# The mixer's last product as two sets of seven block products in place of eight column tiles

## The chip, the cores and the metric

The kernel runs on one core of a Trainium2 chip. The metric is device time in microseconds (us). Of the kernel before, three runs are shown, with a median of 1166.98 us (1166.12 to 1167.22). One further execution, taken with the profiler, lasted 1166.18 us, of which the profile covers a span of 1164.1 us. All places below are in microseconds from the start of that span.

Five engines work side by side, each in the order of its own queue: TensorE (PE, with its weight loads as PEld), VectorE (DVE), ScalarE (ACT), GpSimd (POOL, which here mostly issues adding transfers) and SyncE (SP, which issues most loads). They wait for each other by semaphores.

## The reference

One transformer block over 512 tokens with 1024 features, all in float32: half a SwiGLU feed-forward step, a mixer, another half step, a norm. The mixer is where the change lies:

```python
merged = sigmoid(ga) * y_conv + sigmoid(gb) * y_gla   # y_gla = (...) @ w_out_gla
return merged @ w_o                                   # 512 x 1024 by 1024 x 1024
...
x = x + hybrid_mixer(rmsnorm(x, norm_mix_g), w_in, conv_w, ..., w_o)
x = x + 0.5 * swiglu(rmsnorm(x, norm_ffn2_g), ffn2_w_gu, ffn2_w_down)
```

So the product with w_o is followed at once by the residual sum into x, and by the norm that opens the second feed-forward step (FFN2), whose first product needs that norm's inputs.

## The kernel before, in words

Activations lie transposed: 128 features on the partitions, 512 tokens along the row, so x and the merged tensor are eight tiles of 128x512. To keep float32 accuracy, every operand is split in two float32r parts, high and low, and each product is made of three: high by high, high by low, low by high.

**Weights** come in units of at most 128x1024 through one stream (class `Weights`). `PLAN` lists the units, `STEPS` the order in which the products take them. SP loads a unit from HBM into one of ten slots `f0` to `f9` (`dma`, line 334). Some steps before its use, ACT writes its high part (`wh`, line 374) and DVE its low part (`wl`, line 375); there are three buffers of each. A unit has served when both are written, and its slot can be loaded again. A slot is chosen by the step up to which the slots are needed (`until`).

**Plain tiles.** `mm_group` (line 423) makes four tiles of 128 output features at once, `mm_single` (line 409) one; either way a tile of 128x512 takes 8 blocks of 128 inputs by 3 parts, 24 matmuls with 512 columns. Before the change, the w_o product is one group and then four single tiles, 8 tiles in all. Its operands `m_h`, `m_l` are written by `split_pair` (lines 1560 and 1561) as soon as the merged tensor is ready, its results go through `evac` (line 1662): x = result + the old x, which had been loaded into eight tiles `x_old` during the product with w_out_conv. After each tile `nxt.add` feeds FFN2's norm: ACT writes x times gain as high part (line 459) and the square (465, 468), DVE the low part (460) and the running sum of squares (469).

**Sets.** Most other products are made of sets of seven block products after Strassen and Winograd: the weights of 1024 inputs by 512 outputs are four blocks a11, a12, a21, a22, the operand is four blocks of 4 feature tiles by 256 tokens, and seven products of blocks (named m1, p2, q6, p5, q7, p4, p3) take the place of eight. A narrow product (`Product.narrow`, line 533) is 24 matmuls with 256 columns and takes one unit of weights. The sums of weight blocks are made in place: POOL's adding transfers do a21 += a22 first, a11 += a21 once the weights of m1 have been split, and a12 += a11 once those of p2 have been split; DVE makes s3 = a11 + a21 (line 361). The sums of operand blocks are made by DVE in place (lines 749 to 756), and each is split by `Both` (ACT line 623, DVE line 624, in two halves). The products pile up in three PSUM banks a, b, c per set; where a bank holds a finished quarter of the output, `done` takes it out, and the bank's next product has to wait for that. The product with w_out_gla is of this kind (two sets; the results are taken out by lines 609, 612, 1641 and 1645), and so are FFN2's.

**What sets the order.** The program is written product by product, with the weights of the next two or three steps being split ahead (`Weights(2)`), and with operands made two steps ahead in `run_sets`. A scheduler of the framework then orders each engine's queue; on the chip each engine follows its own.

Of the kernel before, what the change touches and what calls it, by code (L numbers as in the profile page):

```python
# [62 lines left out]
def unit_cols(u):  # L63
    return u[2] * len(u[3]) * u[4]
# [7 lines left out]

HW = 256


# [32 lines left out]

def sets(mat, pairs):
# [41 lines left out]
def mixer_plan():  # L151
# [28 lines left out]
def block_kernel(ctx: ExitStack, tc: tile.TileContext, xT, vecs, gf, gup, wgl, wts, out):  # L180
# [101 lines left out]
    class Weights:  # L282
# [3 lines left out]
        def __init__(self, ahead):  # L286
            self.ahead = ahead
            self.issued = 0
            self.taken = 0
            self.end = 0  # L290
            self.ready = []
            self.raw = {}
            self.loads = {}
            self.sums = {}
            self.first = {}

        def phase(self, early, first=6):


            self.early = early  # L300
            self.until = [-1] * SLOTS
            lo, self.end = self.end, [e for e in ENDS if e > self.end][0]
# [26 lines left out]
        def dma(self, n, until):  # L329
            u = PLAN[n]  # L330
            w = unit_cols(u)
            o = offset(n)
            t = self.slot(until)
            nc.sync.dma_start(t[:, :w], wts[o : o + P * w].rearrange("(p n) -> p n", p=P))
            return t

        def load_set(self, n):
# [16 lines left out]
        def issue(self):  # L354
# [192 lines left out]
    class Set:  # L547
# [52 lines left out]
        def quarter(self, p):  # L600
# [12 lines left out]
            return t  # L613

    class Both:

# [113 lines left out]
    class Operands:  # L730
# [4 lines left out]

        def __init__(self, b):
            self.b = b
            self.parts = {}
            self.sums = set()
# [20 lines left out]
        def make(self, p):  # L760
            if p in self.parts:
                return
            i = self.ORDER.index(p)
            if i > 0:
                self.make(self.ORDER[i - 1])
            v = self.sum(p)
# [377 lines left out]
    def mixer(norm, nxt):  # L1144
# [8 lines left out]

        Y = [tile_of("y", [P, 2, S + 2]) for _ in range(4)]

# [422 lines left out]
        def sigmoid(t):  # L1578
# [3 lines left out]

        c_h, c_l = parts([Y[i][:, :, 2:] for i in range(4)])
        m = [two(d // 2)[:, d % 2] for d in range(KD)]

# [9 lines left out]
        ga = [gate("ga", d) for d in range(2)]  # L1595
        x_old = [QK[2 + i][:, j] for i in range(2) for j in range(2)] + [
            pools["g"].tile([P, S], F32, tag=t, name=f"{t}_x") for t in ("sc", "reset", "gup_w", "glr")]
        gb_new = []
# [5 lines left out]
        for d in range(KD):  # L1604
# [24 lines left out]
        sigmoid(gb_new.pop())  # L1629
        m_h, m_l = [None] * KD, [None] * KD  # L1630

        def gla_done(i):
            def done(s, p):
                if not (i == 1 and p in ("q6", "p5", "q7")):
                    finish_late()
                if p not in QUARTERS:
# [6 lines left out]
                    op0=ALU.mult, op1=ALU.mult)  # L1643
                y = two(d // 2)
                nc.vector.tensor_tensor(out=y[:, :, half(l)], in0=y[:, :, half(l)], in1=pair(g),
                                        op=ALU.add)
# [11 lines left out]
        run_sets(lambda i: Set(oo, gla_done(i)), hooks={(0, "p3"): [reload]})  # L1658
        finish_late()

        def evac(d, o):
            nc.vector.tensor_tensor(out=x[d], in0=o, in1=x_old[d], op=ALU.add)
            nxt.add(d)

        for d, o in enumerate(mm_group("w_o", KD, (0, P, 2 * P, 3 * P), m_h, m_l)):
            evac(d, o)
        for d in range(4, KD - 2):
            evac(d, mm_single("w_o", KD, d * P, m_h, m_l))
        for d, o in [(d, mm_single("w_o", KD, d * P, m_h, m_l)) for d in range(KD - 2, KD)]:
            evac(d, o)  # L1670

    FFN = dict(f=1, hidw=2, hid=3, tp=9)
    with phase("small1", **FFN):
# [10 lines left out]
        ffn("ffn1_w_gu", "ffn1_w_down", n1, nm, PLAIN1, 5)  # L1684
    with phase("small2", f=1, v=4, qk=2, g=1, y=4, small=1):
        W.phase(4, 5)
# [49 lines left out]
```

## Time and profile before

| | |
|---|---|
| time of three runs, median | 1166.98 us |
| profiled execution: time, span | 1166.18 us, 1164.1 us |
| PE busy | 1155.0 us, 99% of the span |
| DVE, ACT, POOL busy | 956.7, 684.6, 117.7 us |
| granted clock of TensorE | 0.999 of full speed |
| w_out_conv (single tiles) | up to 739.14 |
| w_out_gla (14 narrow products) | 739.14 to 779.67 |
| w_o (8 tiles) | 779.67 to 823.21 |
| FFN2 begins | 823.21 |

How to read it: PE is the busy engine, and its rows follow each other nearly without a gap, so a stage lasts as long as its matmuls, plus what PE waits. A matmul's own duration is longer than the step from one to the next, since they are pipelined; steps, not durations, add up. The same holds on DVE and ACT, where an instruction starts a little before the one ahead has ended.

### The profile page before, as it was taken

The numbers are of one execution on the slowest core, as the hardware profiler recorded it, in microseconds if no ns is written. First come the engines' busy times: TensorE is split into PE (matmuls) and PEld (weight loads), VectorE is DVE, ScalarE is ACT, GpSimd is POOL, SyncE is SP. The second block draws the span as 40 slices with busy tenths as digits, with TensorE's granted clock in tenths as the row PEclk, the third lists the DMA queues.
The fourth block names the chain that finished last, engine by engine and source line by source line (L and its number), as shares of the span: only waits on it lengthen the run. The fifth ranks groups of instructions, "written<-read, shape, count | busy, mean of one in ns | idle before, by whom it ended". The sixth has DMA issues, their size and how long they took to land.

```text
span 1164.1 us, 17143 instructions
## 1 busy us (share of the span) xinstructions
PE 1155.0 (99%) x6626; PEld 1016.1 (87%) x6626; DVE 956.7 (82%) x1198; ACT 684.6 (59%) x904; POOL 117.7 (10%) x153
## 2 busy tenths in 40 slices
PE   9999999999999999999999999999999999999997
PEld 7898888988888889999989998998889888898886
DVE  7997888997568977979799998686599788889955
ACT  6466666675335656666666586544356666666443
POOL 0010111101020111100101100000001111111100
PEclk9999999999999999999999999999999999999999
DMA  9388787678524488876868767531738777757721
GB/s 350 79 212 195 178 201 180 163 193 204 207 80 122 106 200 230 197 188 171 224 169 207 211 171 221 134 107 52 227 74 209 182 187 177 196 145 183 184 86 73
DMA packets 62593, 200.11 MB, mean 172 GB/s; under 512 B 6864, under 2 KB 13136, under 8 KB 62512
## 3 DMA queue, kind: packets, MB, share of 16 engines
q1 hardware_dynamic: 39088, 126.37, 32.3%
q0 software_dynamic: 18784, 68.17, 31.8%
q10 hardware_dynamic: 4640, 4.49, 1.1%
q8 instruction: 52, 0.85, 0.3%
q14 instruction: 29, 0.24, 0.1%
HBM read 124.55 MB, written 8.39 MB: 114 GB/s over the span
## 4 chain that ended last, share of the span: by engine, by line
PE 96%; DVE 2%; ACT 1%; DMA 1%; issue 1%; ACTq 0%
PE mm L824 13%; PE mm L409 11%; PE mm L533 11%; PE bb L542 10%; PE z L542 8%; PE mm L423 8%; PE w L542 7%; PE y L542 6%; PE mm L1041 4%; PE aux L824 4%; PE x L542 3%; PE y L533 3%; PE w L533 2%; PE aux L1041 1%; PE z L533 1%; PE x L533 1%
## 5 line engine op out<-in xcount | busy, mean ns | idle before, releaser
L374 ACT CAST wh<-f 128x1024 fp32r<-128x1024 f32 (+1 forms) x341 | 356.0, 1047 | 339.6 <-PE mm L533 37.8
L375 DVE TENSOR_TENSOR wl<-f,wh 128x1024 fp32r<-128x1024 f32 (+1 forms) x341 | 413.6, 1217 | 98.4 <-ACT wh L374 89.3
L352 POOL DMA_DIRECT2D f<-f x126 | 109.0, 865 | 905.8 <-DVE wl L375 512.0
L824 PE MATMUL mm<-wh,op 128*128 128x512 f32 x432 | 106.9, 389 | 0.0
L533 PE MATMUL mm<-op,wh 128*128 128x256 f32 x800 | 105.6, 284 | 0.0
L533 PEld LDWEIGHTS mm<-op,wh 128*128 128x128 f32 x800 | 100.1, 192 | 0.5 <-ACT tp L583 0.2
L542 PE MATMUL bb<-op,wh 128*128 128x512 f32 x384 | 97.9, 395 | 0.0
L824 PEld LDWEIGHTS mm<-wh,op 128*128 128x128 f32 x432 | 80.9, 188 | 16.7
L409 PE MATMUL mm<-op,wh 128*128 128x512 f32 x384 | 91.0, 389 | 0.0
L409 PEld LDWEIGHTS mm<-op,wh 128*128 128x128 f32 x384 | 72.0, 188 | 15.0
L542 PEld LDWEIGHTS bb<-op,wh 128*128 128x128 f32 x384 | 69.4, 189 | 12.7
L542 PE MATMUL z<-op,wh 128*128 128x512 f32 x256 | 64.4, 393 | 0.0
L423 PE MATMUL mm<-op,wh 128*128 128x512 f32 x256 | 64.1, 392 | 0.2 <-DVE op L456 0.2
L824 PE MATMUL mm<-wl,op 128*128 128x512 f32 x216 | 57.7, 389 | 0.0
L423 PEld LDWEIGHTS mm<-op,wh 128*128 128x128 f32 x256 | 47.5, 188 | 10.9 <-ACT wh L374 0.5
L542 PEld LDWEIGHTS bb<-op,wl 128*128 128x128 f32 x384 | 52.3, 190 | 5.0 <-DVE wl L375 1.3
L533 PE MATMUL mm<-op,wl 128*128 128x256 f32 x400 | 56.5, 283 | 0.0
L542 PE MATMUL w<-op,wh 128*128 128x512 f32 x224 | 56.3, 393 | 0.0
L542 PE MATMUL bb<-op,wl 128*128 128x256 f32 x384 | 53.6, 282 | 0.9 <-DVE wl L375 0.9
L542 PEld LDWEIGHTS z<-op,wh 128*128 128x128 f32 x256 | 46.0, 189 | 8.2
L361 DVE TENSOR_TENSOR f<-f,f 128x1024 f32<-128x1024 f32 x42 | 51.3, 1222 | 1.6 <-DMA f<-wts 0.9
L533 PEld LDWEIGHTS mm<-op,wl 128*128 128x128 f32 x400 | 51.8, 192 | 0.3
(334 smaller groups left out, 2003.7 us busy)
## 6 DMA issues: line engine op xcount, KB each, us to landing
f<-wts SPq DMA_DIRECT2D x219, 512.0 KB, 4.5
f<-f POOLq DMA_DIRECT2D x126, 512.0 KB, 5.2
X<-xT SPq DMA_DIRECT2D x8, 256.0 KB, 5.4
xs<-X POOLq DMA_DIRECT2D x8, 256.0 KB, 2.4
tp<-ga SPq DMA_DIRECT2D x8, 256.0 KB, 5.6
y<-tp SPq DMA_DIRECT2D x7, 256.0 KB, 2.0
ga<-tp ACTq DMA_DIRECT2D x6, 256.0 KB, 3.9
gb<-tp ACTq DMA_DIRECT2D x6, 256.0 KB, 3.9
```

Of the source, the lines that this page charges most:

```text
L352: return nc.gpsimd.dma_start(out_, a, accum_op=ALU.add).ins
L361: nc.vector.tensor_tensor(out=s3, in0=a11, in1=a21, op=ALU.add)
L374: self.cast = nc.scalar.copy(h[:, :w], raw[:, :w]).ins
L375: nc.vector.tensor_tensor(out=l[:, :w], in0=raw[:, :w], in1=h[:, :w].bitcast(F32), op=ALU.subtract)
L409: nc.tensor.matmul(o, w[:, i * P : (i + 1) * P], a[k], start=j == k == 0, stop=j == 2 and k == kt - 1)
L423: nc.tensor.matmul(o[c], w[:, s : s + P], a[k], start=k == 0 and j == 0, stop=k == kt - 1 and j == 2)
L533: nc.tensor.matmul(o[:, e * HW : (e + 1) * HW], w[:, k * HW + e * P : k * HW + (e + 1) * P], a(k), start=self.fresh and j == k == e == 0, ...
L542: nc.tensor.matmul(o[:, e, :n], w[:, k * HW + e * P : k * HW + (e + 1) * P], a(k), start=self.fresh and k == 0 and w is self.h, stop=k == ...
L824: nc.tensor.matmul(o[t], a(k)[:, t * P : (t + 1) * P], ww[:, i * 512 : (i + 1) * 512], start=fresh and j == k == 0, stop=j == 2 and k == 3 ...
L1041: nc.tensor.matmul(o[t][e], b if j == 1 else a, wl if j == 2 else wh, start=k == K0 and e == 1 and j == 0, stop=k == KF - 1 and j == 2, sk ...
```

## The change

The w_o product becomes two sets of seven narrow products, of four output feature tiles (512 features) each, run in the same call of `run_sets` as the two sets of w_out_gla. `OUT_SEQ` writes out their order: (0, "m1") is the first product of the set for outputs 0 to 511, (1, "m1") that of the set for 512 to 1023. Both sets share their split operands `mo`, made from the merged tensor `MY`. `Straight` runs a product into its bank, copies b into a new bank a after m1, and hands every product's bank to `out_done`, which adds or subtracts it directly into a quarter of x (`X2`), which has been loaded there from `xs` (`reload`, now 8 loads during w_out_gla). After p3 a set's feature tiles 0 and 1 are complete, after p4 tiles 2 and 3, and `nxt.add` runs for two at a time. s3 is not summed by DVE: SP loads a11 a second time into s3's slot, and POOL adds a21 from HBM to it. Slots' `until` is kept between phases. Y's four tiles become one.

```diff
+BY_DMA = ("w_o",)
...
+OUT_SEQ = ((0, "m1"), (0, "p5"), (1, "m1"), (0, "p2"), (0, "q6"), (1, "p5"), (0, "q7"),
+           (0, "p3"), (0, "p4"), (1, "q6"), (1, "p2"), (1, "q7"), (1, "p3"), (1, "p4"))
...
-    STEPS.extend(order(firsts))
+    STEPS.extend([(firsts[i], p) for i, p in seq] if seq else order(firsts))
...
-    units(group("w_o", KD, (0, P, 2 * P, 3 * P)))
-    for d in range(4, KD):
-        units(single("w_o", KD, d * P))
+    sets("w_o", [(4 * i * P, (4 * i + 2) * P) for i in range(2)], OUT_SEQ)
...
-            s3 = self.slot(a["q7"])
+            s3 = self.dma(n, a["q7"]) if PLAN[n][0] in BY_DMA else self.slot(a["q7"])
...
-                nc.vector.tensor_tensor(out=s3, in0=a11, in1=a21, op=ALU.add)
+                if PLAN[n][0] not in BY_DMA:
+                    nc.vector.tensor_tensor(out=s3, in0=a11, in1=a21, op=ALU.add)
                 self.first[n] = self.add(a21, a22)
+                if PLAN[n][0] in BY_DMA:
+                    self.add(s3, self.block(n + 2))
...
+    class Straight:
+        BANK = {"m1": "b", "p2": "a", "q6": "b", "p5": "c", "q7": "b", "p4": "b", "p3": "c"}
...
+        def run(self, p):
+            n = self.BANK[p]
+            fresh = n not in self.bank
+            if fresh:
+                self.bank[n] = self.new(n)
+            Product(*W.take(), self.group.get(p), fresh).narrow(self.bank[n])
+            if p == "m1":
+                self.bank["a"] = self.new("a")
+                nc.scalar.copy(self.bank["a"], self.bank["b"])
+            self.done(p, self.bank[n])
...
-            nc.sync.dma_start(x_old[d], xs[d])
...
-                if p in ("p4", "p3"):
-                    def f():
-                        for j, (b, c) in enumerate(split_pair(y)):
-                            m_h[d + j], m_l[d + j] = b, c
-                    late.append(f)
...
+            for d in range(KD):
+                nc.sync.dma_start(x[d], xs[d])
+        mo = Operands(
+            lambda j, l: MY[:, 4 * j : 4 * j + 4, half(l)],
+            ("m1", "p5", "p2", "q6", "q7", "p3", "p4"))
+        def out_done(i):
+            def done(p, o):
+                if p == "m1":
+                    return
+                a = int(p in ("p5", "q7", "p4"))
+                l = int(p not in ("p2", "p4"))
+                d = 4 * i + 2 * a
+                v = XS[-1][:, d : d + 2, half(l)]
+                if a:
+                    nc.vector.scalar_tensor_tensor(out=v, in0=pair(o), scalar=-1.0, in1=v,
+                                                   op0=ALU.mult, op1=ALU.add)
+                else:
+                    nc.vector.tensor_tensor(out=v, in0=pair(o), in1=v, op=ALU.add)
+                if p in ("p3", "p4"):
+                    for e in range(2):
+                        nxt.add(d + e)
+            return done
+        def out_bank(i):
+            return lambda n: AUX() if (i, n) == (1, "b") else MM()
...
-        for d, o in enumerate(mm_group("w_o", KD, (0, P, 2 * P, 3 * P), m_h, m_l)):
-            evac(d, o)
-        for d in range(4, KD - 2):
-            evac(d, mm_single("w_o", KD, d * P, m_h, m_l))
-        for d, o in [(d, mm_single("w_o", KD, d * P, m_h, m_l)) for d in range(KD - 2, KD)]:
-            evac(d, o)
+        run_sets(out_set, hooks={(0, "p3"): [reload]})
```

The queues at three places. Line numbers are those of the kernel each row is from: 374, 375 of the kernel before are 384, 385 in the changed one, 459, 460, 468, 469 are 469, 470, 478, 479, and 623, 624 are 655, 656.

**PE at the end of w_o.** Before, the last tile's matmuls end and FFN2's group begins:

```order
L409 MATMUL mm1186_7830<-op1140_7503,wl1183_7772 128x512 x2
L409 MATMUL mm1186_7830<-op1125_7370,wl1183_7772 128x512 x2
L409 MATMUL mm1186_7830<-op1151_7580,wl1183_7772 128x512 x2
L409 MATMUL mm1186_7830<-op1149_7573,wl1183_7772 128x512 x2
L423 MATMUL mm1196_7898<-op1168_7708,wh1200_7902 128x512
```

Now, from the end of the eleventh product (1, p2), whose weights are wh1186 and wl1187 (aux1162 is bank b of the second set, mm1174 its bank c):

```order
L543 MATMUL mm1165_7694<-op1156_7624,wl1187_7874 128x256 x4
L543 MATMUL mm1174_7767<-op1172_7761,wh1194_7944 128x256 x4
L543 MATMUL mm1174_7767<-op1173_7764,wh1194_7944 128x256 x4
L543 MATMUL aux1162_7665<-op1168_7726,wh1192_7915 128x256 x4
L543 MATMUL aux1162_7665<-op1169_7729,wh1192_7915 128x256 x4
```

The first eight matmuls of the thirteenth product (1, p3) stand ahead of the twelfth, (1, q7). They need wh1194, the high part of a12 + a11 of the second set. That sum is the last adding transfer of w_o on POOL, and it can only be issued once wl1187 has been written from the same slot, f1131.

**DVE in the second half of w_o.** Before, at the sixth tile:

```order
L1662 TENSOR_TENSOR X2_7377<-mm1175_7733,sc_x_6749 128x512
L375 TENSOR_TENSOR wl1183_7772<-f1163_7648,wh1182_7771 128x1024
L460 SCALAR_TENSOR_TENSOR op1179_7764<-X2_7377,vec_84,op1178_7763 128x512
L469 TENSOR_TENSOR acc16_7707<-acc16_7707,tp1180_7767 128x512
L1662 TENSOR_TENSOR X2_7377<-mm1181_7770,reset_x_6750 128x512
```

Now, from (0, p3)'s result to (1, q6)'s:

```order
L1699 TENSOR_TENSOR X2_7368<-mm1157_7627,X2_7368 128x2x256
L385 TENSOR_TENSOR wl1187_7874<-f1131_7385,wh1186_7873 128x1024
L470 SCALAR_TENSOR_TENSOR op1184_7864<-X2_7368,vec_84,op1183_7863 128x512
L1696 SCALAR_TENSOR_TENSOR X2_7368<-mm1151_7589,X2_7368 128x2x256
L470 SCALAR_TENSOR_TENSOR op1184_7864<-X2_7368,vec_84,op1183_7863 128x512
L479 TENSOR_TENSOR acc16_7862<-acc16_7862,tp1185_7870 128x512
L385 TENSOR_TENSOR wl1193_7916<-f1130_7383,wh1192_7915 128x1024
L470 SCALAR_TENSOR_TENSOR op1189_7904<-X2_7368,vec_84,op1188_7903 128x512
L479 TENSOR_TENSOR acc16_7862<-acc16_7862,tp1190_7907 128x512
L470 SCALAR_TENSOR_TENSOR op1189_7904<-X2_7368,vec_84,op1188_7903 128x512
L479 TENSOR_TENSOR acc16_7862<-acc16_7862,tp1191_7912 128x512
L1699 TENSOR_TENSOR X2_7368<-aux1162_7665,X2_7368 128x2x256
```

The norm work of feature tiles 0 to 3 now stands in one block between two evacuations of banks.

**ACT from w_o into FFN2.** Before, FFN2's first two weight units (wh1200, wh1203) are cast ahead of the last two tiles' norm work:

```order
L459 ACTIVATE op1178_7763<-X2_7377,vec_84 128x512
L468 ACTIVATE tp1184_7802<-X2_7377 128x512
L374 CAST wh1200_7902<-f1191_7888 128x1024
L374 CAST wh1203_7908<-f1192_7890 128x1024
L468 ACTIVATE tp1189_7860<-X2_7377 128x512
```

Now they (wh1215, wh1218) stand behind the norm work of tiles 4 and 5, which needs the result of the thirteenth product:

```order
L384 CAST wh1194_7944<-f1131_7385 128x1024
L384 CAST wh1196_7973<-f1129_7381 128x1024
L469 ACTIVATE op1198_8027<-X2_7368,vec_84 128x512
L478 ACTIVATE tp1200_8031<-X2_7368 128x512
L469 ACTIVATE op1198_8027<-X2_7368,vec_84 128x512
L478 ACTIVATE tp1201_8036<-X2_7368 128x512
L384 CAST wh1215_8109<-f1206_8095 128x1024
L384 CAST wh1218_8115<-f1207_8097 128x1024
```

The cast of FFN2's first weights has moved from ahead of the last results to behind those of the thirteenth product.

More of the change, by code (lines that the diff above doesn't have):

```diff
@@ L613, in quarter, with __init__ @@
             return t
+    class Straight:
+        BANK = {"m1": "b", "p2": "a", "q6": "b", "p5": "c", "q7": "b", "p4": "b", "p3": "c"}
+        def __init__(self, group_, done, new):
+            self.group = group_
+            self.done = done
+            self.new = new
+            self.bank = {}
+        def run(self, p):
[8 more added lines that the diff above has]
+            self.done(p, self.bank[n])
     class Both:
@@ L1151, in mixer @@
             nc.gpsimd.dma_start(xs[k], x[k])
-        Y = [tile_of("y", [P, 2, S + 2]) for _ in range(4)]
+        YS = tile_of("y", [P, 4, 2, S + 2])
+        Y = [YS[:, i] for i in range(4)]
         def flat(i):
@@ L1583, in mixer @@
         c_h, c_l = parts([Y[i][:, :, 2:] for i in range(4)])
-        m = [two(d // 2)[:, d % 2] for d in range(KD)]
+        MY = YS.rearrange("p i e t -> p (i e t)")[:, : KD * S].rearrange("p (d t) -> p d t", t=S)
+        m = [MY[:, d] for d in range(KD)]
         n64 = [front.tile([P, HEADS * 16], F32, tag=t, name=f"{t}o") for t in
@@ L1595, in mixer @@
         ga = [gate("ga", d) for d in range(2)]
-        x_old = [QK[2 + i][:, j] for i in range(2) for j in range(2)] + [
-            pools["g"].tile([P, S], F32, tag=t, name=f"{t}_x") for t in ("sc", "reset", "gup_w", "glr")]
         gb_new = []
@@ L1656, in reload, with out_set @@
             x[:] = [XS[-1][:, k] for k in range(KD)]
[L1658 to L1663, printed above, removed]
-        for d, o in enumerate(mm_group("w_o", KD, (0, P, 2 * P, 3 * P), m_h, m_l)):
-            evac(d, o)
-        for d in range(4, KD - 2):
-            evac(d, mm_single("w_o", KD, d * P, m_h, m_l))
-        for d, o in [(d, mm_single("w_o", KD, d * P, m_h, m_l)) for d in range(KD - 2, KD)]:
-            evac(d, o)
+            for d in range(KD):
[22 more added lines that the diff above has]
+            return lambda n: AUX() if (i, n) == (1, "b") else MM()
+        def out_set(i):
+            if i < 2:
+                return Set(oo, gla_done(i))
+            return Straight(mo, out_done(i - 2), out_bank(i - 2))
+        run_sets(out_set, hooks={(0, "p3"): [reload]})
     FFN = dict(f=1, hidw=2, hid=3, tp=9)
@@ L1684, in block_kernel @@
         ffn("ffn1_w_gu", "ffn1_w_down", n1, nm, PLAIN1, 5)
-    with phase("small2", f=1, v=4, qk=2, g=1, y=4, small=1):
+    with phase("small2", f=1, v=4, qk=2, g=1, y=1, small=1):
         W.phase(4, 5)
```

28 lines of the change are left out of this document (14 added, 14 removed).

## The prediction

> **What bounds the kernel now.** I read the page's busy times first, then its chain that ended last.
>
> ```profile
> PE 1155.0 (99%) x6626; PEld 1016.1 (87%) x6626; DVE 956.7 (82%) x1198; ACT 684.6 (59%) x904; POOL 117.7 (10%) x153
> ...
> PE 96%; DVE 2%; ACT 1%; DMA 1%; issue 1%; ACTq 0%
> ```
>
> PE works for 99% of the span and makes 96% of the chain, so a change pays by what it takes from PE, less the waits that PE gets for it. Next, stretches of the program: engines' busy time, granted clock, DMA share and GB/s, for w_out_gla, for w_o, and for the mixer's earlier sets.
>
> ```profile
> core 0: us, PE busy (x) PEld busy (x) DVE busy (x) ACT busy (x) POOL busy (x), PEclk, DMA share, GB/s
> 739.10:779.70 40.60, 40.60 (x338) 40.39 (x338) 32.14 (x39) 21.33 (x27) 1.72 (x2) 1.00 0.54 148
> 779.70:823.20 43.50, 43.50 (x194) 36.02 (x193) 28.02 (x35) 19.08 (x25) 0.00 (x0) 1.00 0.30 109
> 640.00:699.00 59.00, 59.00 (x400) 54.73 (x399) 55.73 (x72) 41.46 (x53) 4.31 (x5) 1.00 0.70 189
> ```
>
> The clock is full in all three. In w_o DVE is idle for 15.5 of 43.5 us, POOL does nothing, and DMA is busy for 0.30. The last row matters too: sets kept DVE busy for 55.73 of 59 us there, and PE never stopped.
>
> **What the change takes from PE.** Rows of PE (start, duration) at both borders of w_o:
>
> ```profile
> 776.79 2.08 PE L533 MATMUL mm<-op,wh 128*128 128x256 f32 x16
> 778.71 1.12 PE L533 MATMUL mm<-op,wl 128*128 128x256 f32 x8
> 779.67 2.00 PE L423 MATMUL mm<-op,wh 128*128 128x512 f32 x8
> ...
> 801.45 3.79 PE L409 MATMUL mm<-op,wh 128*128 128x512 f32 x16
> 805.08 1.98 PE L409 MATMUL mm<-op,wl 128*128 128x512 f32 x8
> 806.89 3.79 PE L409 MATMUL mm<-op,wh 128*128 128x512 f32 x16
> 810.52 1.98 PE L409 MATMUL mm<-op,wl 128*128 128x512 f32 x8
> ...
> 823.21 1.98 PE L423 MATMUL mm<-op,wh 128*128 128x512 f32 x8
> ```
>
> A narrow product takes 779.67 − 776.79 = 2.88 us (24 matmuls, 120.0 ns apart), a plain tile 806.89 − 801.45 = 5.44 (226.7 ns apart). w_o goes from 823.21 − 779.67 = 43.54 = 8 × 5.44 to 14 × 2.88 = 40.32: **−3.22 us** if PE never waits. Not −5.44, as seven for eight would give: half the columns take more than half the time.
>
> The Trainium skill (TensorE: Matmul & The Clock Gate, section "Wait — 56ns, not 53.3ns?") gives a warm start-to-start of N ÷ 2.4 GHz plus about 2.5 ns: 109.2 and 215.8 ns here, so 336 × 109.2 = 36.7 against 192 × 215.8 = 41.4, and −4.7 us. The trace has 120.0 and 226.7, so the sum goes by the rows.
>
> **What it adds elsewhere.** Each unit of w_o's weights that is multiplied is split: 8 before, 14 now, so 6 more casts on ACT and 6 more low parts on DVE. The operands (8 splits of one tile before) are sums and `Both` splits now, and 12 results go into x where 8 did. All this lies beside PE's 40 us except where PE catches up with it. I looked for these places along the queues, from what is done at the border.
>
> **Stall 1, ahead of the thirteenth product (1, p3).** Its first eight matmuls stand ahead of the twelfth, and need the cast of a12 + a11. That sum is issued after wl1187 on DVE. DVE's steps, and the chain from an adding transfer to its cast, by the trace of before:
>
> ```profile
> 774.46 0.68 DVE L609 SCALAR_TENSOR_TENSOR tp<-mm,tp 128x512 f32<-128x512 f32 x1
> 775.18 0.69 DVE L1641 SCALAR_TENSOR_TENSOR g<-tp,g 128x512 f32<-128x512 f32 x1
> ...
> 779.33 1.21 DVE L375 TENSOR_TENSOR wl<-f,wh 128x1024 fp32r<-128x1024 f32 x1
> 780.46 0.68 DVE L1645 TENSOR_TENSOR y<-y,g 128x512 f32<-128x512 f32 x1
> 781.06 0.68 DVE L612 TENSOR_TENSOR tp<-mm,tp 128x512 f32<-128x512 f32 x1
> ...
> 804.87 0.75 DVE L460 SCALAR_TENSOR_TENSOR op<-X,vec,op 128x512 fp32r<-128x512 f32 x1
> 805.53 0.69 DVE L469 TENSOR_TENSOR acc<-acc,tp 128x512 f32<-128x512 f32 x1
> ```
>
> ```profile
> 767.37 0.86 POOL L352 DMA_DIRECT2D f<-f  x1 [16.71 <-DVE wl L375]
> 772.24 1.05 ACT L374 CAST wh<-f 128x1024 fp32r<-128x1024 f32 x1 [3.02 <-DMA f<-f]
> ```
>
> A step of 1024 columns is 780.46 − 779.33 = 1.13 us, one of 512 is 781.06 − 780.46 = 0.60 (0.72 where it reads what the one ahead wrote: 775.18 − 774.46), a norm low part 805.53 − 804.87 = 0.66. The instruction at 774.46 (the result of q7 of w_out_gla's second set) is the same in both kernels. From it up to and with wl1187, DVE's changed queue has 40 instructions: 14 of 1024 (11 low parts of weights, 3 operand sums) and 26 of 512 (10 that finish the GLA quarters, 10 low halves of operands, 6 evacuations). 14 × 1.13 + 26 × 0.60 = 31.42, plus 0.12 for the one dependent pair and 0.09 since the last counts with its whole 1.22: 774.46 + 31.63 = 806.09 if DVE never waits. PE has then 5.26 us left: eleven products end at 779.67 + 11 × 2.88 = 811.35.
>
> How long the add takes is the open price. Issue to landing in the trace (the last number; first the page's medians, with the loads of x beside them, then two single adds):
>
> ```profile
> f<-f POOLq DMA_DIRECT2D x126, 512.0 KB, 5.2
> X<-xT SPq DMA_DIRECT2D x8, 256.0 KB, 5.4
> ...
> f<-f POOLq DMA_DIRECT2D x1, 512.0 KB, 4.5
> ...
> f<-f POOLq DMA_DIRECT2D x1, 512.0 KB, 8.7
> ```
>
> The adds' median is 5.2; 4.5 is one at 861.6, in FFN2, and 8.7 one at 702.8, among the mixer's sets. The pair of rows above gives 772.24 − 767.37 = 4.87. I take the median: 806.09 + 5.2 + 1.05 (cast) + 0.04 = 812.38, a stall of **1.03 us**. Lower bound: with 4.5 the cast is ready at 811.68, but behind these eight matmuls (0.96) the twelfth product waits for its bank, which DVE frees behind wl1187, four norm low parts, one more weight part and four steps of 512: 806.00 + 4 × 0.66 + 1.13 + 4 × 0.60 + 0.69 = 812.86, against 811.35 + 0.96 = 812.31. So at least 0.55 even with a quick add. Upper bounds: with 8.7, 815.88 and 4.5 us; or, if every DVE instruction took its duration (1.22, 0.68) and not its step, 14 × 0.09 + 26 × 0.08 = 3.3 more, 4.4 us. The nearest row for the steps is the window 640 to 699, where DVE ran dense without a stall of PE; so the steps hold.
>
> **Stall 2, at FFN2's first matmul.** It waits for the cast wh1215, now behind the norm work of tiles 4 and 5, which need the thirteenth product's result. That chain, in rows of before (DVE, then ACT):
>
> ```profile
> 812.53 0.69 DVE L1662 TENSOR_TENSOR X<-mm,reset_x 128x512 f32<-128x512 f32 x1 [0.33 <-PE mm L409]
> ```
>
> ```profile
> 801.71 0.72 ACT L459 ACTIVATE op<-X,vec 128x512 fp32r<-128x512 f32 x1
> 802.33 0.62 ACT L465 ACTIVATE acc<-X 128x512 f32<-128x512 f32 x1
> 802.85 0.71 ACT L459 ACTIVATE op<-X,vec 128x512 fp32r<-128x512 f32 x1
> 803.46 0.62 ACT L468 ACTIVATE tp<-X 128x512 f32<-128x512 f32 x1
> 803.98 0.71 ACT L459 ACTIVATE op<-X,vec 128x512 fp32r<-128x512 f32 x1
> ...
> 813.26 0.72 ACT L459 ACTIVATE op<-X,vec 128x512 fp32r<-128x512 f32 x1 [2.17 <-DVE X L1662]
> ```
>
> A product's last matmul ends 778.71 + 1.12 − 779.67 = 0.16 after the next could start; its result reaches DVE 0.03 later (812.53 against 810.52 + 1.98); evacuation 0.69; 0.04 to ACT (813.26 against 812.53 + 0.69); four activations 803.98 − 801.71 = 2.27 (0.03 more for the last one's end); cast 1.05; 0.03 to PE. Sum 4.30, less the fourteenth product's 2.88 that covers it: **1.42 us**. Before, this cast stood ahead of the last results and cost nothing. Bounds: if DVE is one weight part (1.13) late at the evacuation, 2.55; without the 0.16 of tail, which the trace only models, and with every activation at its shortest step, 802.85 − 802.33 = 0.52, so 0.19 less for the four, 1.07. The queues fix the rest.
>
> The last product's own result is no such place: tiles 6 and 7 are the last two of FFN2's eight input blocks, six blocks of 12 matmuls at 226.7 ns (16 us) behind its start.
>
> **The transfers.** x comes by 8 loads of 256 KB on SP during w_out_gla, in the place of 8 equal ones into `x_old`. The first quarter of x is read only after the second of w_o's products (785.4), and DMA is idle for 0.46 of w_out_gla's time, so I count them, and the weight loads behind them on SP, as hidden by that stage's 40 us; without that cover the first evacuation would wait for a landing, 5.4 us in the row of the other loads of this size.
>
> s3 is loaded again, and POOL adds a21 to it from HBM; the trace has no such add. It stands in POOL's queue ahead of a11 += a21 of its set, which q6, the fifth product, needs at 779.67 + 4 × 2.88 = 791.2. Both follow the split of m1's weights, which I put at the weight part next ahead of w_o's start:
>
> ```profile
> 777.59 1.22 DVE L375 TENSOR_TENSOR wl<-f,wh 128x1024 fp32r<-128x1024 f32 x1
> ```
>
> If the second add only runs when the first has landed: 778.81 + 5.2 + 5.2 + 1.05 + 0.04 = 790.3, no wait; with one of the two at 8.7, 793.8, a wait of 2.6. I take 0 of 0 to 2.6, since the median leaves 0.9 and POOL has no row in this stretch of before.
>
> **The sum.** −3.22 + 1.03 + 1.42 = −0.77. On the profiled execution's 1166.18 that is 1165.4 (2.1 of it outside the span of 1164.1); on the median of the runs, which is 0.80 higher, **1166.2**. Two of the three microseconds that PE saves go back as waits for an engine that was idle before.
>
> **Rivals.** A measurement of this kernel can tell about 0.2% (2.33 us) from no change; so faster is below 1164.65, slower above 1169.31.
>
> *The whole gain comes through.* The adds land early and DVE is ahead: 1166.98 − 3.22 = 1163.8. For it: window 640 to 699. Against it: both counts would have to be wrong, and stall 2's has measured rows alone. Chance 0.10.
>
> *The last add comes late.* One mechanism: (1, p3)'s a12 + a11 goes out late on POOL and lands in 8.7, in place of 5.2. Stall 1 is then 4.5, the sum −3.22 + 4.5 + 1.42 = +2.7, 1169.7. It decides from a landing of 6.0 (no gain left) and 8.3 (visibly slower). For it: the row of 8.7, and PE has nothing else to do, since the twelfth product stands behind. Against it: DMA is busy for 0.30 in w_o, 0.70 in the window shortly before that 8.7. Chance 0.17.
>
> *The add from HBM blocks POOL's queue.* With a landing of 8.7 for one of the two, the fifth product waits 2.6: −0.77 + 2.6 = +1.8, 1168.8. For it: two adds issued one behind the other, in a form with no row. Against it: the idle queues of w_o. Chance 0.06.
>
> *The narrow step is shorter than it looks*, by the rule above as a mechanism of the array: its 4.7 in place of 3.22 would leave −4.7 + 2.45, 1164.7. The 24-matmul rows deny it. Chance 0.02.
>
> **How the numbers follow.** My forecast, both stalls near their size, has 0.65: 1166.2, its own range 1165.4 (both stalls at their lower bounds, 0.55 and 1.07) to 1167.3 (stall 2 at its upper, 2.55). Faster: 0.10, half of the 0.02, and a tail of 0.04 of the forecast: 0.15. Slower: of the late add's 0.17 the larger part, 0.12, a third of the HBM add's 0.06, and 0.03 of the forecast, where both stalls come out at their upper bounds: 0.17. Same is left, 0.68. The range reaches from the whole gain, 1163.8, to the late add, 1169.7.
>
> **What would show it.** PE: 14 products of 2.88, with about 42.8 us from w_out_gla's end to FFN2; one gap near 1.0 ahead of (1, p3), put down to the ACT cast, which itself waited for the DMA f<-f; one gap near 1.4 at FFN2's first group, put down to ACT wh. DVE: hardly idle from 774 to 812. If DVE idles while PE waits, the count is wrong and the add is the cause. If PE waits at the fifth product, it is POOL's queue; if between w_out_gla's end and the first product, the merged operands, for which I have no stall.

## The result and the profile after

The changed kernel takes 1172.16 us (median of 6 runs, 1171.6 to 1174.17), the kernel before, in 6 runs beside them, 1166.39. The ratio is 1.0051, with a 95% interval from 1.0038 to 1.0064: **slower by 5.8 us**, where 0.8 us faster was forecast, and outside the range.

The profiled execution took 1174.17 us, its span is 1172.5. What PE waited for, first in the kernel before, then in the changed one (us in total, times, longest):

```profile
PE aux L267 <- POOL ones L264: 1.1, 1, 1.1
PE bb L542 <- DVE wl L375: 0.9, 1, 0.9
PE mm L423 <- DVE op L456: 0.2, 1, 0.2
```

```profile
PE mm L543 <- ACT tp L593: 3.9, 1, 3.9
PE y L543 <- ACT tp L722: 1.5, 2, 0.8
PE mm L433 <- ACT wh L384: 1.3, 1, 1.3
...
PE mm L543 <- ACT wh L384: 1.0, 1, 1.0
```

The rows of 1.3 and 1.0 us are the two waits of the forecast. (This view counts from the modelled end of the matmul before; from step to step a wait is about 0.16 longer.) The first one, 3.9 us for a copy on ACT, is new. PE's rows of the changed kernel show where it lies, and where the forecast ones lie:

```profile
774.24 1.12 PE L543 MATMUL mm<-op,wl 128*128 128x256 f32 x8
779.28 3.49 PE L543 MATMUL mm<-op,wh 128*128 128x256 f32 x16 [3.92 <-ACT tp L593]
782.58 1.34 PE L543 MATMUL mm<-op,wl 128*128 128x256 f32 x8
783.76 2.08 PE L543 MATMUL mm<-op,wh 128*128 128x256 f32 x16
...
786.64 2.08 PE L543 MATMUL mm<-op,wh 128*128 128x256 f32 x16
...
817.80 1.12 PE L543 MATMUL mm<-op,wl 128*128 128x256 f32 x8
819.96 1.21 PE L543 MATMUL mm<-op,wh 128*128 128x256 f32 x8 [1.03 <-ACT wh L384]
...
827.72 1.12 PE L543 MATMUL aux<-op,wl 128*128 128x256 f32 x8
830.10 2.11 PE L433 MATMUL mm<-op,wh 128*128 128x512 f32 x8 [1.25 <-ACT wh L384]
```

w_out_gla now runs from 740.34 to 786.64, w_o from there to 830.10. So the new wait is not in w_o at all: it stands in front of the thirteenth of w_out_gla's own fourteen products, which the change did not touch. The sixteen matmuls behind it take 782.58 − 779.28 = 3.30 us in place of 1.92, 206 ns apart in place of 120: the clock had dropped, to 0.50 of full speed in the microsecond from 780 on. The windows of the changed kernel show that (the columns are those of the windows above):

```profile
740.30:786.60 46.30, 42.32 (x337) 41.88 (x337) 34.66 (x44) 21.76 (x30) 4.32 (x6) 0.96 0.81 220
786.60:830.10 43.50, 41.04 (x339) 40.46 (x337) 38.78 (x52) 25.21 (x37) 4.34 (x5) 1.00 0.57 154
775.00:780.00 5.00, 1.08 (x8) 0.88 (x7) 1.22 (x2) 2.30 (x3) 0.62 (x1) 0.97 0.77 201
780.00:781.00 1.00, 1.00 (x7) 1.00 (x6) 0.96 (x3) 0.18 (x1) 0.24 (x1) 0.50 0.82 254
780.00:785.00 5.00, 5.00 (x33) 5.00 (x32) 4.96 (x9) 1.75 (x3) 0.24 (x1) 0.69 0.95 238
```

By stages:

| | before | after | difference |
|---|---|---|---|
| w_out_gla | 40.53 | 46.30 | +5.77 |
| w_o | 43.54 | 43.46 | −0.08 |
| ahead of w_out_gla | 739.14 | 740.34 | +1.20 |
| from FFN2 on | 340.89 | 342.40 | +1.51 |

The last two rows belong in part to this one execution, the slowest of the six. The second row of the waits is 1.5 us in FFN1 and FFN2, which the change leaves alone. It comes and goes between profiled executions: of the runs below, before_burst, s3_dve, after_half and mended have none of it, like the kernel before, and the other five have 0.2 to 1.4 us. The other five executions of the changed kernel took 1171.6 to 1172.6. What is left is w_out_gla's 5.77 less 0.08, and the medians differ by 5.77.

**Why ACT's copy came late.** The chain, in rows of the changed kernel (POOL, ACT), and one row of the kernel before that answers to the copy:

```profile
750.99 0.86 POOL L359 DMA_DIRECT2D f<-f  x1 [12.91 <-DVE wl L385]
753.32 0.86 POOL L359 DMA_DIRECT2D f<-f  x1 [1.47 <-DMA f<-wts]
...
771.69 0.86 POOL L359 DMA_DIRECT2D f<-f  x1 [7.90 <-DVE wl L385]
```

```profile
761.48 1.05 ACT L384 CAST wh<-f 128x1024 fp32r<-128x1024 f32 x1 [5.96 <-DMA f<-f]
...
777.70 1.04 ACT L384 CAST wh<-f 128x1024 fp32r<-128x1024 f32 x1 [4.00 <-DMA f<-f]
778.65 0.58 ACT L593 COPY tp<-mm 128x512 f32<-128x512 f32 x1
```

```profile
773.19 0.58 ACT L583 COPY tp<-mm 128x512 f32<-128x512 f32 x1
```

The adding transfer of 750.99 is w_out_gla's own a11 += a21 of its second set. It landed in 10.4 us; its twin in the kernel before, issued at 749.79, in 4.8. So the cast of 761.48 came 4.6 us late (before, it ran at 755.65, and 1.2 us of shift are to be added), DVE's low parts behind it came late, and the add of 771.69, a12 + a11 for the last product, went out 3.1 us late (768.57 would be the answer to 767.37) and took 5.9 us. ACT's cast of that sum waits for it, and behind that cast in ACT's queue stands the copy that takes q7's result out of its bank. The thirteenth product writes that bank.

In the kernel before, the copy ended at 773.77 and the thirteenth product began at 773.82. From that last add to PE the chain had no slack at all. Further up it had some: the first add landed 5.6 us later than before, the last one was issued 3.1 us late, and with 1.1 us more of landing PE lost about 4.

What the transfers did from 745 to 760, first before, then after (median us to landing last):

```profile
f<-wts SPq DMA_DIRECT2D x3, 512.0 KB, 4.2
f<-f POOLq DMA_DIRECT2D x1, 512.0 KB, 4.8
```

```profile
f<-wts SPq DMA_DIRECT2D x4, 512.0 KB, 6.7
X<-xs SPq DMA_DIRECT2D x8, 256.0 KB, 5.4
f<-f POOLq DMA_DIRECT2D x2, 512.0 KB, 10.7
```

The eight loads of x went out in a burst, 746.5 to 754.7, around the add of 751. w_o's first add (753.32) and weights also came into this stretch. Which of them did the harm was to be tested.

### The profile page after: what moved, and what is told of

Read it like the earlier page. It is cut to its first block, busy times and chain, and to the rows that moved or that the text cites. A ratio compares the mean times of both kernels' runs of the same rounds, so it can differ in the third digit from the quotient of the medians.

```text
span 1172.5 us, 17524 instructions
## 1 busy us (share of the span) xinstructions
PE 1154.3 (98%) x6770; PEld 1022.5 (87%) x6770; DVE 973.0 (83%) x1222; ACT 693.5 (59%) x922; POOL 124.6 (11%) x161
## 5 line engine op out<-in xcount | busy, mean ns | idle before, releaser
L384 ACT CAST wh<-f 128x1024 fp32r<-128x1024 f32 (+1 forms) x347 | 361.7, 1047 | 335.8 <-DMA f<-f 38.7
L385 DVE TENSOR_TENSOR wl<-f,wh 128x1024 fp32r<-128x1024 f32 (+1 forms) x347 | 420.2, 1215 | 96.3 <-ACT wh L384 91.5
L359 POOL DMA_DIRECT2D f<-f x132 | 114.5, 868 | 891.6 <-DVE wl L385 525.9
L543 PE MATMUL mm<-op,wh 128*128 128x256 f32 x960 | 128.2, 286 | 5.2 <-ACT tp L593 3.9
L543 PEld LDWEIGHTS mm<-op,wh 128*128 128x128 f32 x960 | 121.2, 193 | 6.3 <-ACT tp L593 4.1
L419 PE MATMUL mm<-op,wh 128*128 128x512 f32 x320 | 75.8, 389 | 0.0
L419 PEld LDWEIGHTS mm<-op,wh 128*128 128x128 f32 x320 | 60.0, 188 | 12.5
L543 PE MATMUL mm<-op,wl 128*128 128x256 f32 x480 | 67.9, 284 | 0.0
L543 PEld LDWEIGHTS mm<-op,wl 128*128 128x128 f32 x480 | 62.4, 193 | 0.3
L433 PE MATMUL mm<-op,wh 128*128 128x512 f32 x192 | 48.2, 393 | 1.4 <-ACT wh L384 1.3
L552 PE MATMUL y<-op,wh 128*128 128x512 f32 x192 | 48.3, 393 | 0.0
```

The lines of the kernel that those rows point to most:

```text
L359: return nc.gpsimd.dma_start(out_, a, accum_op=ALU.add).ins
L384: self.cast = nc.scalar.copy(h[:, :w], raw[:, :w]).ins
L385: nc.vector.tensor_tensor(out=l[:, :w], in0=raw[:, :w], in1=h[:, :w].bitcast(F32), op=ALU.subtract)
L419: nc.tensor.matmul(o, w[:, i * P : (i + 1) * P], a[k], start=j == k == 0, stop=j == 2 and k == kt - 1)
L433: nc.tensor.matmul(o[c], w[:, s : s + P], a[k], start=k == 0 and j == 0, stop=k == kt - 1 and j == 2)
L543: nc.tensor.matmul(o[:, e * HW : (e + 1) * HW], w[:, k * HW + e * P : k * HW + (e + 1) * P], a(k), start=self.fresh and j == k == e == 0, ...
```

## The experiments

Theory A: the burst of the loads of x makes w_out_gla's add late. Theory B: w_o's own transfers do. In both, the lateness gets to PE through the copy that stands behind the cast. All ratios are to the kernel before, run beside on the same chip (medians 1166.55 to 1166.58).

**old_x: the loads of x go back to where they were.** The first result of each quarter is then summed with the old x from its eight tiles.

```diff
...
+            nc.sync.dma_start(x_old[d], xs[d])
...
-            for d in range(KD):
-                nc.sync.dma_start(x[d], xs[d])
...
+                if p in ("q7", "p3"):
+                    old = [(v, pair(o), v)]
+                elif i == 0:
+                    old = [(v, pair(o), QK[2 + a][:, :, half(l)])]
+                else:
+                    old = [(v[:, e], pair(o)[:, e], x_old[d + e][:, half(l)]) for e in range(2)]
...
```

> The changed kernel with one part undone: the old x is loaded into eight tiles during w_out_conv, as before the change, and the first result of each quarter is added to it from there (twelve more or less: four more DVE instructions). Theory A (the burst of eight loads of x at 746 to 755 makes the adding transfer issued at 751 land in 10.4 us in place of 4.8, and that lateness reaches PE at w_out_gla's thirteenth product as 3.9 us of idling and 1.6 us at a lower clock): that adding transfer lands in at most 6 us, no wait above 0.5 at that product, granted clock 1.00 from 770 to 790; the two waits of the forecast (1.0 and 1.3) stay; about 1165.9, 6 us under the changed kernel. Theory B (w_o's own transfers, the adding one at 753 and s3's from HBM at 763, are what collides): the adding transfer still takes 8 us or more, the wait stays above 2.5, 1170 to 1172.

Measured: 1168.01 us, ratio 1.0010 [1.0001, 1.0018]. The add landed in 4.5 us, nothing waited in w_out_gla, and the clock stayed at 1.00. So theory A's chain is undone. But it was 2 us slower than expected. Two waits came in w_o that the changed kernel had not shown at that size, ahead of the seventh product (799.02) and of the ninth (806.10):

```profile
PE mm L543 <- DVE X L1707: 1.1, 1, 1.1
PE mm L543 <- DVE X L1704: 1.1, 1, 1.1
```

Of the two waits of the forecast, the one ahead of (1, p3) is gone in return. So w_o took 824.95 − 780.49 = 44.46 us, 1.0 longer than in the changed kernel, which is half of the 2 us. In the profiled execution, which is 1 us above the median, 1.4 us more are the wait in FFN1 and FFN2.

**before_burst: the loads alone, in the kernel before.**

```diff
...
-            nc.sync.dma_start(x_old[d], xs[d])
...
             x[:] = [XS[-1][:, k] for k in range(KD)]
+            for d in range(KD):
+                nc.sync.dma_start(x[d], xs[d])
...
-            nc.vector.tensor_tensor(out=x[d], in0=o, in1=x_old[d], op=ALU.add)
+            nc.vector.tensor_tensor(out=x[d], in0=o, in1=x[d], op=ALU.add)
```

> The kernel before with one part of the change alone: x is loaded by eight loads during w_out_gla into the place of the result, and the results of the plain w_o tiles are added there. Theory A: the adding transfer issued at 749.8 lands in 8 us or more (4.8 before), PE waits 1.5 to 4 us at w_out_gla's thirteenth product, 1168 to 1171. Theory B: it lands in 6 us or less, no wait there, 1166.4 as before.

Measured: 1173.52 us (1169.44 to 1175.33), ratio 1.0062 [1.0049, 1.0076]. The plain w_o, with nothing but eight loads moved, is as slow as the changed kernel, and slower than the range I had written down. In the profiled execution, the fastest of the five, the transfers from 745 to 760 and PE's wait were:

```profile
X<-xs SPq DMA_DIRECT2D x8, 256.0 KB, 5.3
f<-wts SPq DMA_DIRECT2D x3, 512.0 KB, 8.8
f<-f POOLq DMA_DIRECT2D x1, 512.0 KB, 11.1
```

```profile
772.72 1.12 PE L533 MATMUL mm<-op,wl 128*128 128x256 f32 x8
777.02 2.17 PE L533 MATMUL mm<-op,wh 128*128 128x256 f32 x16 [3.18 <-ACT tp L583]
779.03 1.12 PE L533 MATMUL mm<-op,wl 128*128 128x256 f32 x8
```

The add landed in 11.1 us, more than in the changed kernel, with none of w_o's adds beside it. Theory A stands, and theory B is not needed for the wait. The wait of 3.18 is followed by matmuls at full speed (779.03 − 777.02 = 2.01 us for sixteen), and this execution's mean granted clock is 0.999; the other four took 1172.6 to 1175.3 us, with 0.995.

**copy_first: the copy ahead of the cast.** All transfers stay; ACT's cast of w_out_gla's last weights is queued behind the copy.

```diff
...
-            self.cast = nc.scalar.copy(h[:, :w], raw[:, :w]).ins
+            with (tc.issue_after(self.behind.pop(at)) if at in self.behind else ExitStack()):
+                self.cast = nc.scalar.copy(h[:, :w], raw[:, :w]).ins
...
-                    nc.scalar.copy(v, o)
+                    c = nc.scalar.copy(v, o).ins
+                    n, q = STEPS[W.taken - 1]
+                    if q == "q7" and PLAN[n][0] == "w_out_gla" and STEPS[W.taken][1] == "p2":
+                        W.behind[W.taken + 2] = c
```

> The changed kernel with one order changed on ACT: the copy that takes q7's result out of its bank (second set of w_out_gla) is queued ahead of the cast of the last product's weights, not behind it. The transfers stay as they are. If the copy stuck behind a cast that waits for an adding transfer is the link between the late transfer and PE: the thirteenth product no longer waits, the fourteenth waits at most 1 us for the cast itself, no drop of the clock, 1167 to 1168. If PE's wait has another cause, it stays at 3 to 4 us and the time at 1172.

Measured: 1168.26 us, ratio 1.0015 [1.0006, 1.0024]. ACT's rows:

```profile
760.50 1.05 ACT L386 CAST wh<-f 128x1024 fp32r<-128x1024 f32 x1 [6.12 <-DMA f<-f]
...
772.64 0.57 ACT L595 COPY tp<-mm 128x512 f32<-128x512 f32 x1
776.01 2.95 ACT L386 CAST wh<-f 128x1024 fp32r<-128x1024 f32 x3 [2.79 <-DMA f<-f]
```

The add is as late as ever (10.5 us to landing), ACT still waits for it at 760.5 and for the last product's add at 776.0, but the copy is done at 773.2, and PE waited neither at the thirteenth product nor at the fourteenth. Two rows of ACT's queue in the other order are worth about 4 us here. The link is shown. The time is slightly above the range: in w_o a wait of 1.3 us came at the seventh product, as in old_x. But the order on POOL that old_x_s3 tests, below, is not its cause. Here a11 += a21 of w_o's first set was issued at 780.95, ahead of the second set's s3 (786.65), so that POOL's order differs from the changed kernel's too; it landed in 7.6 us all the same. Why was not tested.

**s3_dve: s3 by DVE, no transfers for it.**

```diff
-BY_DMA = ("w_o",)
+BY_DMA = ()
```

> The changed kernel with s3 made by DVE as before: no second load of a11 and no adding transfer from HBM. Theory A: the adding transfer at 751 still lands in 8 us or more, the wait at w_out_gla's thirteenth product is 2.5 to 4 us; 1170 to 1173. Theory B, as far as s3's transfers are the cause: the wait is gone, 1166 to 1168.

Measured: 1170.88 us, ratio 1.0038 [1.0026, 1.0051]. The add at 750.4 landed in 10.3 us, PE waited 3.9, and the clock fell (its rows are in the last section). So s3's transfers are not what makes w_out_gla's add late. In w_o they are another matter (old_x_s3).

**burst_half: half of the burst, in the kernel before.** Tiles 0 to 3 of x as before the change, tiles 4 to 7 by four loads during w_out_gla.

```diff
...
-            nc.sync.dma_start(x_old[d], xs[d])
+            if d < 4:
+                nc.sync.dma_start(x_old[d], xs[d])
...
+            for d in range(4, KD):
+                nc.sync.dma_start(x[d], xs[d])
...
```

> The kernel before with half of the burst: x's tiles 4 to 7 are loaded by four loads during w_out_gla into the place of the result, tiles 0 to 3 as before the change. If the number of bytes in the burst sets how late the adding transfer of 749 lands (4.8 us without, 11.1 with eight loads): it lands in 6 to 9 us, PE waits 0.3 to 2 us at the thirteenth product of w_out_gla, the clock stays at 1.00, 1166.8 to 1168.5. If any load there does the whole harm: 10 us or more, a wait of 3 us, 1169 to 1174.

Measured: 1166.18 us, ratio 1.0000 [0.9991, 1.0009]. The transfers from 745 to 760:

```profile
X<-xs SPq DMA_DIRECT2D x4, 256.0 KB, 4.9
f<-f POOLq DMA_DIRECT2D x1, 512.0 KB, 5.8
```

The add landed in 5.8 us, PE did not wait. Both cases I had written down were wrong: the harm does not grow with the bytes from the first load on. 1 MB more in that stretch cost one microsecond of landing, 2 MB more (before_burst) cost six.

**after_half: the same half, in the changed kernel.**

```diff
...
-            for d in range(KD):
+            for d in range(4, KD):
                 nc.sync.dma_start(x[d], xs[d])
...
+                w = v if i or p in ("q7", "p3") else QK[2 + a][:, :, half(l)]
...
```

> The changed kernel with half of the burst: tiles 0 to 3 of the old x are loaded during w_out_conv, tiles 4 to 7 by four loads during w_out_gla; on DVE no instruction more. In the kernel before, half of the burst let the adding transfer land in 5.8 us and cost nothing. If w_o's own transfers add little to that: the adding transfer of 751 lands in 5 to 7 us, a wait of at most 1 us at w_out_gla's thirteenth product, full clock, 1166 to 1168 (the waits of w_o as in old_x). If the bytes of both sum up past what that stretch bears: it lands in 8 us or more, a wait of 2 to 4 us, 1169 to 1172.

Measured: 1167.35 us, ratio 1.0015 [1.0005, 1.0025]. The add landed in 8.3 us and the thirteenth product waited 1.7:

```profile
PE mm L543 <- ACT tp L593: 1.7, 1, 1.7
```

It lies between the two cases: with half of the burst, w_o's own transfers do count, 8.3 against 5.8 us of landing and a wait of 1.7 against none. Without the loads they cost nothing (4.5 in old_x), and beside the whole burst nothing more (10.4 against 11.1 in before_burst). So theory B has a share, but only with loads of x there. The full clock held. Two of the twelve executions took 1171.6 and 1172.5, with a mean granted clock of 0.997 and 0.995; there is no trace of them.

**old_x_s3: the order of POOL's queue in w_o.** In old_x, POOL issued a11 += a21 of w_o's first set at 781.94, behind the adding transfer from HBM for the second set's s3 (781.37). It landed in 7.5 us, and ACT waited 5.4 for it (cast at 789.55). Here s3's transfer is issued behind a11 += a21 of its own set.

```diff
...
-                if PLAN[n][0] in BY_DMA:
-                    self.add(s3, self.block(n + 2))
...
-                self.add(a11, a21, self.first[twin])
+                ins = self.add(a11, a21, self.first[twin])
+                if PLAN[n][0] in BY_DMA:
+                    self.add(s3, self.block(n + 2), ins)
```

> The kernel old_x with s3's adding transfer from HBM queued on POOL behind a11 += a21 of its set, not ahead of it. In old_x POOL held a11 += a21 of w_o's first set until 781.9, behind the transfer for the second set's s3, it landed in 7.5 us, and PE waited 1.1 us twice in w_o for results that DVE took out late. If that queue is the cause: a11 += a21 goes out at 777 to 780, both waits fall under 0.4 us, a wait near 1.0 us ahead of (1, p3) comes back in part; 1166.3 to 1167.3. If DVE's load alone is the cause: both waits stay, 1168.

Measured: 1166.03 us, ratio 0.9995 [0.9985, 1.0005], 2 us under old_x, and a little under the range expected. a11 += a21 went out at 780.27 and landed in 5.9 us. What PE waited for in w_o and behind it:

```profile
PE mm L433 <- ACT wh L382: 1.3, 1, 1.3
...
PE mm L543 <- DVE X L1704: 0.6, 1, 0.6
```

One of the two waits is gone and the other nearly halved, to more than the 0.4 us expected, by the order of a queue alone; the wait ahead of (1, p3) did not come back. That the rest is DVE's load was not tested by itself.

**mended: all of it together.** old_x, old_x_s3 and copy_first, and two orders against the two waits of the forecast: (1, p2) stands ahead of (1, q6), so that the last add of w_o can go out earlier, and the norm work of tiles 2 to 7 is issued behind the cast of FFN2's first weights. The lines of these two orders:

```diff
...
-            (0, "p3"), (0, "p4"), (1, "q6"), (1, "p2"), (1, "q7"), (1, "p3"), (1, "p4"))
+            (0, "p3"), (0, "p4"), (1, "p2"), (1, "q6"), (1, "q7"), (1, "p3"), (1, "p4"))
...
-                if p in ("p3", "p4"):
+                if p in ("p3", "p4") and d < 2:
...
+        for k in range(2, KD):
+            if k < 3:
+                W.issue()
+            n2.add(k)
```

> All mends together: old x loaded during w_out_conv, s3's transfer behind a11 += a21, the copy of q7 ahead of the cast of w_out_gla's last weights, (1, p2) ahead of (1, q6), and the norm work of tiles 2 to 7 behind the cast of FFN2's first weights. If the named waits are all that stood against the 3.2 us that PE saves: no wait of PE over 0.5 us between 739 and FFN2's group, 1163.0 to 1164.3. If DVE is a bound in w_o whatever the order: one to two microseconds of waits stay, 1164.5 to 1166.

Measured: **1163.75 us, ratio 0.9976 [0.9965, 0.9987]**: 2.8 us faster than the kernel before, of 3.22 that PE saves, and it beats both kernels; that is the first case. The waits of PE, all of them (the first two are in the kernel before as well):

```profile
PE aux L270 <- POOL ones L267: 1.1, 1, 1.1
PE bb L554 <- DVE wl L385: 0.9, 1, 0.9
PE aux L545 <- DVE X L1712: 0.4, 1, 0.4
```

The two new orders were not run by themselves, so what each of them is worth is open.

**mended_burst: the same with x's burst left in.** The diff is that of mended without the lines of old_x.

> The same without the first mend: x is still loaded by eight loads in a burst during w_out_gla. If the burst only harms through the copy that stood behind the cast: within 1 us of the run mended. If late transfers find other ways to PE: 1.5 to 4 us above it, with the adding transfer of 750 landing in about 10 us in both cases.

Measured: 1166.50 us, ratio 1.0007 [0.9998, 1.0015], 2.75 above mended. The add of 749.41 landed in 9.8 us. The copy no longer stands in the way, but two other waits came:

```profile
PE aux L545 <- DVE X L1704: 1.4, 1, 1.4
PE mm L545 <- ACT wh L384: 1.3, 1, 1.3
```

So the lateness that the burst makes is still there when w_o begins (POOL issued a11 += a21 of its first set at 780.27, in mended at 777.43), and finds other ways to PE. Moving the loads is the cure, the order of the copy is a stopgap.

## Why the prediction was wrong

**The step that failed is the one on the transfers**: "so I count them, and the weight loads behind them on SP, as hidden by that stage's 40 us; without that cover the first evacuation would wait for a landing". I asked whether the moved loads would be there in time. They were: the last landed at 765, more than 20 us ahead of the first use. What I did not ask is whom they would delay. The cover I named was a mean, DMA idle for 0.46 of 40 us. In the stretch into which the eight loads fell, it was the other way round (before, then after):

```profile
745.00:755.00 10.00, 10.00 (x86) 10.00 (x85) 6.84 (x9) 4.32 (x6) 0.86 (x1) 1.00 0.71 182
```

```profile
745.00:755.00 10.00, 10.00 (x86) 10.00 (x85) 6.88 (x9) 4.67 (x6) 1.72 (x2) 1.00 0.84 288
755.00:765.00 10.00, 9.94 (x83) 9.74 (x82) 5.65 (x8) 4.04 (x7) 0.87 (x1) 1.00 1.05 279
```

DMA was busy for 0.71 already. It came to 0.84 with the loads, and to 1.05 in the ten microseconds behind, where the kernel before has 0.40 (a share in this view can pass 1). Two terms that I had put at nothing came of it, a wait and a drop of the clock in w_out_gla. The loads are issued by SP and the adds by POOL, and still one delayed the other. The Trainium skill (DMA: Bandwidth & Descriptors, section "Issuing engines are not separate DMA queues") says that transfers end up on the same 16 DMA engines and interleave, whichever engine issued them. The runs agree: 4.8 us to landing without the burst, 11.1 with it and nothing else.

**The row that would have told it stood in the prediction**: ACT's cast at 772.24 with "3.02 <-DMA f<-f". I used it to price an adding transfer. It also says that ACT was waiting for one, in w_out_gla, with a copy behind it that PE needs, and that PE began 0.05 us after that copy. Every microsecond by which that add is issued or lands later shows. I looked for such places only in the stage that the change rewrites.

**"The last add comes late" had the right mechanism at the wrong place.** The rival put a landing of 8.7 at w_o's last add. That add landed in 4.5. The late one was of w_out_gla, 60 us earlier. I had given this rival 0.17; no case of mine held what happened, and so none of the chance lay there. The two other rivals are out: the gain did not come through, and the narrow step is 120 ns as before.

**The matmuls: right.** A narrow product is 2.88 us in the changed kernel as before it (786.64 − 783.76), and 14 of them take 40.32.

**Stall 1: right, 1.20 us for a forecast 1.03.** Eleven products of w_o ended at 817.80 + 0.96 = 818.76, and the next matmul began at 819.96. Its working holds only in part. The add landed in 4.5 and not in 5.2, but POOL issued it 0.3 later than DVE's low part ended, for which I had put nothing, and DVE had 4.8 us in hand and not 5.26. The clock and the waits ahead had shifted PE and DVE against each other, so that the closeness is partly luck.

**Stall 2: right, 1.42 for 1.42**, from 827.72 + 0.96 = 828.68 to 830.10; FFN2's first matmul waited for the cast of its weights, as was said. In mended, where that cast stands ahead of the norm work, the wait is gone.

**POOL's queue: right that it costs, not how.** I took 0 of 0 to 2.6 us for the transfers from HBM ahead of a11 += a21, and let the second run only when the first has landed. They overlap: in old_x the two went out at 781.37 and 781.94 and landed in 5.6 and 7.5 us. The fifth product never waited. What came late was a bank that DVE had to free: in the changed kernel only 0.33 us at the seventh product (804.25), in old_x two waits of 1.1 at the seventh and the ninth. Turning the order (old_x_s3) took 2 us off.

**What the sum would have been** with the two missing terms: −3.22 + 1.20 + 1.42 + 0.33, and in w_out_gla 4.08 for the wait (779.28 − 775.20) and 1.60 for the clock (4.48 − 2.88), is +5.4; the medians say +5.8.

## What to carry to other kernels

When a change moves transfers, ask whom they delay where they now go, in windows of a few microseconds and not by a stage's mean, and look first at transfers that an engine already waits for. A full window is a warning and no more: 0.97 cost nothing in burst_half. A wait in the trace that costs PE nothing has to be followed to the instruction behind it in the same queue: with no slack there, a late transfer reaches PE at once. Queue what frees a bank ahead of what waits for a transfer, and queue an add that is due soon ahead of one that is due late.

## What the runs showed of the hardware

**PE's clock fell after two waits of 3.9 us, and not after one of 3.2.** In the changed kernel 3.92 us without a matmul were followed by sixteen in 3.30 us, in s3_dve 3.88 by sixteen in 782.14 − 778.56 = 3.58, where 1.92 is usual; 3.18 in before_burst and 1.66 in after_half were followed by full speed. Read in windows of 0.2 us, the granted clock was 0.50 from about 779.7 to 783.1 in the changed kernel and from about 777.5 to 784.3 in s3_dve: 3.4 us, and twice that. In the one it fell 0.4 us after PE had begun again, in the other 1.1 us before. So a wait that is a little longer cost 1.6 us more at once in the changed kernel, and 2.4 in s3_dve (24 matmuls in 783.84 − 778.56 = 5.28, for 2.88):

```profile
778.56 3.78 PE L543 MATMUL mm<-op,wh 128*128 128x256 f32 x16 [3.88 <-ACT tp L593]
782.14 1.91 PE L543 MATMUL mm<-op,wl 128*128 128x256 f32 x8
783.84 0.41 PE L543 MATMUL mm<-op,wh 128*128 128x256 f32 x1
```

The Trainium skill (TensorE: Matmul & The Clock Gate, section "What's actually happening") says that the clock goes to half after one idle window of about 3.4 us, and that the window runs free. The four runs agree with that figure, and the two lengths of the half clock with one and two such windows. Four waits do not show whether every longer wait brings the drop. A prediction of a stall near that length should carry the drop as a term of its own.

**The landing of an adding transfer is not proportional to what goes on beside it.** 1 MB more of loads added one microsecond (4.8 to 5.8), 2 MB more added six (to 11.1). Why the second megabyte costs so much more was not tested. The DMA share from 745 to 755 was 0.97 with the half burst and 0.90 with the whole one, so the share does not tell the two apart. The loads also stood nearer to the add in the second case: SP issued the last one 0.6 us ahead of it (748.6 and 749.2), with the half burst 2.7 us (747.1 and 749.8). Bytes and nearness were not separated.
